# One power on GpSimd for each inverse square root, a new emission order, and other splits on GpSimd, in a fused decoder layer

## The chip, the cores and the metric

The kernel runs on one core of one Trainium2 chip. The metric is the device time of one execution in microseconds (us). The kernel before was timed in three runs: median 384.21 us, from 383.61 to 385.0.

## What is computed

One decoder layer for 256 tokens of width 1024, in fp32, cut to its steps:

```python
h = rmsnorm(x, attn_norm)                       # x: 256 x 1024
mq, mk, mv, gqkv, gz, ga, gb = split(h @ w_in)  # seven 512-wide groups, plus 8 columns
y_a = moba_attention(mq, mk, mv)                # 8 heads x 64, causal
gq, gk, gv = split(silu(causal_depthwise_conv(gqkv, conv_w)))
gq, gk = l2norm(gq) * 128**-0.5, l2norm(gk)     # l2norm: x * rsqrt(sum(x*x) + 1e-6)
o = gated_delta_rule(gq, gk, gv, log_decay, beta)   # 4 heads x 128, chunks of 64
y_b = rmsnorm(o, gdn_norm) * silu(gz)
x = x + concat(y_a, y_b) @ w_out
h = rmsnorm(x, ffn_norm)
y = hierarchical_moe(h)   # top-1 of 4 groups, top-2 of its 8 experts, gated MLP, width 256
out = rmsnorm(x + y, final_norm)
```

With 32 experts of 3 MiB the expert weights are 96 MiB; they are all read, once.

## The kernel before

**First part.** The input projection is computed with the weights cut in two fp32r halves. A weight tile of 128 x 2048 is loaded into a 1-MiB buffer; a split step S0 to S71 then takes 512 of its columns: ScalarE casts the high half (L512), and the low half is raw weight minus high half, one subtraction on VectorE or on GpSimd (L514). A string `LOW` has a letter for each split, V or G, that says which. Steps P0 to P55 are the products: each does three passes of four 128x256 matmuls (high weights by high input, high by low, low by high; L536, or L545 for one group). X.h0 to X.h7 make the two halves of the scaled input, ScalarE the high one (L432). X.d0 to X.d4 are warm-up products on zeros (L257, each lowered to two matmuls). The last sixteen splits, S56 to S71, cut the four tiles of w_out, and W0 to W7 are the output projection: 192 matmuls of 128x256 (L1209), of which each W reads its own tile half.

**Between them** stand the steps of the two mixers: the convolutions (gk, gq, gv), the norms (X.rs, K.rs, Q.rs), the inverse of the chunk matrices (I0 to I5), the recurrence (u, kv, s, p, r), its output norm and gate (ON, OG), the scores and softmax of attention (sc, sm, pt, pv). Each inverse square root of a norm is `rsqrt_steps` (L269 to L294): a bit trick and two Newton-like steps, ten or so small VectorE instructions. Users are X.rs (two chains of one column), K.rs and Q.rs (8 columns), ON0 and ON1 (`onorm`, 4 columns) and R.rs (two chains of one column). The last norm of the kernel already uses a single power instruction on GpSimd instead (L1784).

**Routing.** After the residual (X2.0 to X2.3, L1216) come the router's logits (R.lg), the ranks and one-hot choices (R.rt), the inverse root (R.rs), the dispatch matrix (M.D: `make_D` L1372, `scale_D` L1382, both 128x256 on VectorE), and the gather of the tokens for the first group (M.g, L1390). M.p is the gate product of the first group of experts (L1406).

**Experts.** Eight groups of four experts follow; for each, gate, up and down weights come in 1-MiB loads on SyncE's queue, in order, into the buffers that the first part leaves. `load_expert` issues a load where the last step that uses a buffer is emitted. One of these buffers, K1, also holds the two tiles t1x, which belong to the ring t1k of small work tiles; a step takes the ring's first free tile.

**What sets the order.** The string `ORDER` is written by hand: each word advances one step to its next yield, and so fixes the order of the instructions on every engine's own queue. Each engine runs its queue in order. Nothing reorders it afterwards.

## Time and profile before

| | us |
|---|---|
| median of 3 runs | 384.21 |
| the profiled execution | 384.3 |
| its span in the trace | 382.6 |
| TensorE (PE) busy in the span | 335.0 (88%) |
| VectorE (DVE) busy | 192.5 (50%) |
| ScalarE (ACT) busy | 105.6 (28%) |
| GpSimd (POOL) busy | 65.2 (17%) |
| moved by DMA | 123.54 MB, 322 GB/s over the span |

Shares of the whole span say little here, since the first part (up to about 170 us) and the experts have different limits; the views below go by stretch. "Idle before" in a row is the time for which the engine stood still ahead of that row's first instruction, with the instruction that ended it. Names of work tiles are those of the buffers that they share: a weight tile may be called RG, K, B, mixA or whl.

### The profile page before, as it was taken

To read this page: it belongs to the slowest core of one execution; us is meant where nothing else is said; L and a number is where in the kernel's file an instruction comes from. 1 tells how busy PE (TensorE), PEld (TensorE's weight loads), DVE (VectorE), ACT (ScalarE), POOL (GpSimd) and SP (SyncE) were. 2 spreads that over 40 slices of the span, in tenths; PEclk is the share of its full clock that TensorE was granted. 3 is DMA by queue.
4 is the path that set the end of the run, shared out by engine and by line. 5 is a ranking of instruction groups with operands and counts; after the bars stand their busy time and mean duration, and the time that the engine had idled before them with its cause. 6 is when DMAs were issued, how large, how long until landed. Compare 5 with 4: busy or idle time off the path is not lost.

```text
span 382.6 us, 8189 instructions
## 1 busy us (share of the span) xinstructions
PE 335.0 (88%) x3410; PEld 257.8 (67%) x3410; DVE 192.5 (50%) x494; ACT 105.6 (28%) x260; POOL 65.2 (17%) x106
## 2 busy tenths in 40 slices
PE   3999999999999989899969899898987697578980
PEld 2999998987878879799755656465553254254550
DVE  2798889989687876436331313223230121051543
ACT  4664555626632452304001010101010001001032
POOL 5416040630572033400000000000000000000033
PEclk9999999999999999998999999999999699899997
DMA  6979454494303856969999999999999999999952
GB/s 215 423 289 368 173 218 182 164 370 169 111 0 118 325 191 256 409 270 408 386 408 424 421 420 416 420 421 423 419 421 420 421 423 420 421 416 421 421 207 110
DMA packets 18326, 123.54 MB, mean 323 GB/s; under 512 B 2288, under 2 KB 2544, under 8 KB 3824
## 3 DMA queue, kind: packets, MB, share of 16 engines
q1 hardware_dynamic: 18288, 123.01, 79.6%
q8 instruction: 27, 0.44, 0.5%
q14 instruction: 11, 0.09, 0.1%
HBM read 121.95 MB, written 1.05 MB: 322 GB/s over the span
## 4 chain that ended last, share of the span: by engine, by line
PE 45%; DMA 42%; DVE 6%; ACT 2%; issue 1%; POOL 1%; POOLq 0%; SPq 0%; DVEq 0%; ACTq 0%
PE bank L536 18%; DMA EX<-in_w_up_dram 10%; PE bank L1209 6%; DMA hL<-in_w_gate_dram 5%; DMA whl<-in_w_down_dram 5%; DMA mixB<-in_w_down_dram 5%; DMA EX<-in_w_gate_dram 5%; DMA B<-in_w_dl_dram 5%; DMA B<-in_w_gate_dram 5%; PE bank L545 3%; PE bank L1406 3%; PE bank L1390 2%; PE bank L886 1%; PE bank L906 1%; PE bank L1700 1%
## 5 line engine op out<-in xcount | busy, mean ns | idle before, releaser
L1406 PE MATMUL bank<-EX,B2a 128*32 128x256 f32 x416 | 42.8, 396 | 5.0 <-DMA EX<-in_w_up_dram 3.6
L1406 PE MATMUL bank<-B,B2a 128*32 128x256 f32 x240 | 42.2, 395 | 3.3 <-DMA B<-in_w_gate_dram 3.3
L1705 ACT CAST B2b<-bank 128x256 fp32r<-128x256 f32 (+1 forms) x33 | 12.1, 366 | 118.8 <-PE bank L1700 104.4
L1745 POOL TENSOR_TENSOR K<-K,whl 128x256 f32<-128x256 f32 (+1 forms) x10 | 5.9, 624 | 208.4 <-DMA mixB<-in_w_dl_dram 207.4
L536 PE MATMUL bank<-hH,whl 128*128 128x256 f32 x192 | 32.5, 294 | 4.7 <-ACT whl L512 4.7
L1706 DVE TENSOR_TENSOR B2b<-bank,B2b 128x256 fp32r<-128x256 f32 (+1 forms) x33 | 13.8, 417 | 36.2 <-ACT B2b L1705 29.4
L536 PE MATMUL bank<-hL,whl 128*128 128x256 f32 x192 | 31.9, 290 | 0.0
L536 PEld LDWEIGHTS bank<-hH,whl 128*128 128x128 f32 x192 | 27.3, 197 | 6.2 <-ACT whl L512 5.6
L1406 PEld LDWEIGHTS bank<-EX,B2a 128*32 128x32 f32 x416 | 20.6, 114 | 15.2 <-DMA EX<-in_w_up_dram 4.5
L1700 PE MATMUL bank<-B,t1k 128*32 128x512 f32 (+1 forms) x104 | 26.6, 564 | 2.5 <-DVE t1k L1688 1.8
L1390 PE MATMUL bank<-t1k,B 128*128 128x128 f32 x224 | 26.9, 278 | 1.4 <-DVE t1k L1382 1.4
L1390 PEld LDWEIGHTS bank<-t1k,B 128*128 128x128 f32 x224 | 25.5, 192 | 3.8 <-issue 2.1
L536 PEld LDWEIGHTS bank<-hL,whl 128*128 128x128 f32 x192 | 26.9, 196 | 0.9 <-issue 0.8
L1406 PE MATMUL bank<-K,B2a 128*32 128x256 f32 x144 | 25.9, 404 | 1.7 <-DMA K<-in_w_up_dram 1.7
L1712 PEld LDWEIGHTS bank<-B2b,t1k 128*128 128x128 f32 x132 | 18.2, 188 | 12.3 <-ACT B2b L1705 5.9
L1712 PE MATMUL bank<-B2b,t1k 128*128 128x256 f32 (+1 forms) x132 | 24.5, 311 | 1.1
L1612 DVE TENSOR_TENSOR t1k<-t1k,late 128x256 f32<-128x256 f32 x8 | 3.4, 426 | 43.2 <-PE bank L1610 43.2
L1406 PEld LDWEIGHTS bank<-B,B2a 128*32 128x32 f32 x240 | 18.7, 113 | 8.8 <-DMA B<-in_w_gate_dram 4.3
L1393 DVE TENSOR_TENSOR B2a<-bank,late 128x512 f32<-128x512 f32 x16 | 11.1, 692 | 19.8 <-PE bank L1390 19.8
L512 ACT CAST whl<-RG 128x512 fp32r<-128x512 f32 x30 | 17.7, 614 | 9.2 <-DMA RG<-in_w_in_dram 3.7
L1659 DVE SCALAR_TENSOR_TENSOR t1k<-t1k,late,bank 128x256 f32<-128x256 f32 x8 | 3.8, 480 | 29.5 <-PE bank L1406 29.5
L514 DVE TENSOR_TENSOR mixA<-RG,whl 128x512 fp32r<-128x512 f32 x22 | 16.4, 763 | 2.8 <-ACT whl L512 2.8
(391 smaller groups left out, 767.5 us busy)
## 6 DMA issues: line engine op xcount, KB each, us to landing
EX<-in_w_up_dram SPq DMA_DIRECT2D x16, 1024.0 KB, 18.8
B<-in_w_gate_dram SPq DMA_DIRECT2D x11, 1024.0 KB, 19.3
B<-in_w_down_dram SPq DMA_DIRECT2D x11, 1024.0 KB, 19.8
EX<-in_w_gate_dram SPq DMA_DIRECT2D x10, 1024.0 KB, 10.6
EX<-in_w_down_dram SPq DMA_DIRECT2D x6, 1024.0 KB, 19.9
B<-in_w_in_dram SPq DMA_DIRECT2D x5, 1024.0 KB, 5.0
RG<-in_w_in_dram SPq DMA_DIRECT2D x5, 1024.0 KB, 4.8
K<-in_w_gate_dram SPq DMA_DIRECT2D x5, 1024.0 KB, 19.9
```

The costliest lines, as they stand in the source:

```text
L512: S.copy(out=hv, in_=src)
L514: (G if LOW[i] == "G" else V).tensor_tensor(out=lv, in0=src, in1=hv.bitcast(FP32), op=ALU.subtract)
L536: PE.matmul(o_, lhsT=a_[:, c4, j * P:(j + 1) * P], rhs=b_[:, c, :], start=(c == 0 and j % 2 == 0 and n == 0), stop=(c == KC - 1 and j % 2 ...
L545: PE.matmul(ps[tt], lhsT=a_[:, c, tt * P:(tt + 1) * P], rhs=b_[:, c4, :], start=(c == 0 and n == 0), stop=(c == KC - 1 and n == 2))
L1209: PE.matmul(o_, lhsT=a_[:, c, :], rhs=b_, start=(i == 0 and c % 2 == 0 and n == 0), stop=(i == 7 and c % 2 == 1 and n == 2), skip_group_ch ...
L1390: PE.matmul(ps[:, c4 * P:(c4 + 1) * P], lhsT=x2[tt][:, q * 4 + c4, :], rhs=Dsv[:, tt], start=(tt == 0), stop=(tt == 1))
L1393: V.tensor_tensor(out=xeT[:, q * 4:q * 4 + 4, :], in0=ps.rearrange("p (c s) -> p c s", c=4), in1=ffnT[:, q * 4:q * 4 + 4].unsqueeze(2).bro ...
L1406: PE.matmul(ps[r, 0:FF], lhsT=xeT[:, c, r], rhs=w[c // 2][0][:, c % 2, q, :] if mixed else w[q][0][:, c, :], start=(c == 0), stop=(c == KC ...
L1700: PE.matmul(ps[r, 0:w], lhsT=hv[:, ft, r], rhs=rhs, start=(ft == 0), stop=(ft == 1), tile_position=(0, q * 32))
L1705: S.copy(out=hi, in_=ps)
L1706: V.tensor_tensor(out=lo, in0=ps, in1=hi.bitcast(FP32), op=ALU.subtract)
L1712: PE.matmul(ps[tt][:, 0:w], lhsT=DwT[:, tt * P:(tt + 1) * P], rhs=ye[k], start=(first and k == 0), stop=(grp >= NG - 2 and k == 1), skip_g ...
```

## The change

1. `rsqrt_steps` and its interleaver are gone. `inv_root(dst, v, n)` takes their place: one power with exponent -0.5 on GpSimd, of 128 x n values. X.rs and R.rs do both columns in one instruction (n = 2), K.rs and Q.rs have n = 8, ON0 and ON1 n = 4 each. Of VectorE's queue 477 rows become 412 (some rows stand for two or more instructions).
2. `ORDER` is another string: other places for nearly all steps ahead of the experts. The five warm-ups X.d all stand ahead of the first product; E0 to E5, which load expert weights into spare buffers, come at other places, E1 among them.
3. `LOW` has 23 letters G in the place of 14.
4. Routing takes its small tiles with `take(True)`, which skips the two tiles t1x in K1.

```diff
-LOW = "VVVVVVVVVVVVVVVVVVVVVVVVVVVVGVVVVVVVVVGGVGVGGGVVVVVVVGGGVVVVVGVVVGGGVVVV"
+LOW = "VVVVVVVVVVVVVVVVVVGVVVVVVVVVVVVGVGGVVVVGVGGGGVGGGVVGVGGVGVVVGVGGVGGVVVGG"
...
-        def take(self):
+        def take(self, own=False):
             assert self.q, "no free buffer"
-            return self.q.popleft()
+            i = 0
+            while own and any(self.q[i] is b for b in t1x):
+                i += 1
+            t = self.q[i]
+            del self.q[i]
+            return t
...
-    def rsqrt_steps(dst, v, n, sml=None):
...
+    def inv_root(dst, v, n):
+
+        G.tensor_tensor(out=dst, in0=v, in1=mhalf.broadcast_to([P, n]), op=ALU.pow)
...
-        yield from inter(*[rsqrt_steps(rstd[:, tt:tt + 1], ssq[:, 3 + tt:4 + tt], 1) for tt in range(2)])
+        inv_root(rstd, ssq[:, 3:5], 2)
...
-        yield from inter(rsqrt_steps(rk, ssk, 8))
+        inv_root(rk, ssk, 8)
...
-        yield from inter(rsqrt_steps(rq, ssn, 8))
+        inv_root(rq, ssn, 8)
...
-            yield from inter(rsqrt_steps(ro, mo, 4))
+            inv_root(ro, mo, 4)
...
-        for tt in range(2):
-            V.tensor_scalar(out=ss2[:, 2 * tt:2 * tt + 1], in0=ss2[:, 2 * tt:2 * tt + 1], scalar1=1e-6, scalar2=None, op0=ALU.add)
-            yield
-        yield from inter(*[rsqrt_steps(rs2[:, tt:tt + 1], ss2[:, 2 * tt:2 * tt + 1], 1, LATE) for tt in range(2)])
+        ms2 = ss2.rearrange("p (t q) -> p t q", q=2)[:, :, 0]
+        V.tensor_scalar(out=ms2, in0=ms2, scalar1=1e-6, scalar2=None, op0=ALU.add)
+        yield
+        inv_root(rs2, ms2, 2)
```

(`take(True)` stands in R.k, `rank`, R.rt, `make_D` and `scale_D`.)

Line numbers of the changed kernel are lower by some 29 past `inv_root`. On TensorE's queue the start of the kernel before is this (L257 is the warm-up, one row for two matmuls; L536 a product of P0):

```order
L257 MATMUL bank_67<-EX_95 128x256
L257 MATMUL bank_68<-EX_95 128x256
L257 MATMUL bank_69<-EX_95 128x256
L536 MATMUL bank_70<-hH,whl_100 128x256 x2
L536 MATMUL bank_71<-hH,whl_100 128x256 x2
L536 MATMUL bank_70<-hL,whl_100 128x256 x2
```

and of the changed kernel (L261 the warm-up, L507 the product):

```order
L261 MATMUL bank_67<-EX_95 128x256
L261 MATMUL bank_68<-EX_95 128x256
L261 MATMUL bank_69<-EX_95 128x256
L261 MATMUL bank_70<-EX_95 128x256
L261 MATMUL bank_71<-EX_95 128x256
L507 MATMUL bank_72<-hH,whl_100 128x256 x2
L507 MATMUL bank_73<-hH,whl_100 128x256 x2
```

Two warm-ups moved up from later places between products, so that five stand in front.

On GpSimd's queue around the output projection, the kernel before has the last output norm work (L1144), the low half of a mixer output (L1093), the router's scaled weights (L1272) and four splits of w_out (L514):

```order
L1144 TENSOR_TENSOR K_58<-K_58,K_60 128x512 x2
L1093 TENSOR_TENSOR mixA<-B2b,mixA 128x4x128 x2
L1272 TENSOR_TENSOR B_82<-K_60,late 128x288
L514 TENSOR_TENSOR whl_101<-K_59,whl_101 128x512
L514 TENSOR_TENSOR whl_100<-RG_89,whl_100 128x512
L514 TENSOR_TENSOR whl_101<-RG_89,whl_101 128x512 x2
```

and the changed kernel, with L271 the power, L485 the split, L1064 the mixer output, L1243 the router's weights and L1256, L1258 routing constants:

```order
L271 TENSOR_TENSOR K_60<-K_60,late 128x4 x2
L1115 TENSOR_TENSOR K_58<-K_58,K_60 128x512
L485 TENSOR_TENSOR B_1578<-RG_89,B_1578 128x512
L1064 TENSOR_TENSOR mixA<-B2b,mixA 128x4x128 x2
L1243 TENSOR_TENSOR B_82<-K_60,late 128x288
L485 TENSOR_TENSOR whl_101<-K_59,whl_101 128x512
L485 TENSOR_TENSOR B_1660<-K_59,B_1660 128x512 x2
L1256 MEMSET t1k_77 128x64
L485 TENSOR_TENSOR whl_101<-RG_89,whl_101 128x512
L485 TENSOR_TENSOR whl_100<-RG_89,whl_100 128x512
L1258 AFFINE_SELECT t1k_77<-t1k_77 128x64
L485 TENSOR_TENSOR whl_100<-K_59,whl_100 128x512 x2
```

Behind the mixer's output, four splits became seven, and one stands ahead of it.

On SyncE's queue, the loads of the second group's experts begin in the kernel before with

```order
L473 DMA B_80<-in_w_down_dram 128x2048 [waits DMAHW2_49,DVE_49]
L473 DMA K_60<-in_w_down_dram 128x2048 [waits DMAHW3_49]
L470 DMA K_58<-in_w_gate_dram 128x2048 [waits DMAHW4_49,DVE_49,PE_49]
L470 DMA B_79<-in_w_gate_dram 128x2048 [waits DMAHW5_49,PE_49]
```

and in the changed one with

```order
L444 DMA B_80<-in_w_down_dram 128x2048 [waits DMAHW2_49,DVE_49]
L444 DMA K_60<-in_w_down_dram 128x2048 [waits DMAHW3_49]
L441 DMA K_58<-in_w_gate_dram 128x2048 [waits DMAHW4_49]
L441 DMA B_79<-in_w_gate_dram 128x2048 [waits DMAHW5_49,PE_49]
```

The load into K1 (K_58) lost its waits for VectorE and TensorE; the load behind it kept its wait.

## Rows read from the trace of the kernel before

**Rows 1.** By stretch: busy PE, PEld, DVE, ACT, POOL (instructions), PE clock, DMA share, GB/s.

```profile
9.00:53.00 44.00, 44.00 (x358) 43.13 (x359) 35.86 (x94) 23.95 (x51) 13.23 (x35) 1.00 0.76 300
...
61.00:112.00 51.00, 50.97 (x630) 44.50 (x629) 44.13 (x107) 25.28 (x62) 21.01 (x20) 1.00 0.48 186
...
204.00:369.00 165.00, 139.37 (x1512) 84.09 (x1514) 43.49 (x95) 14.91 (x42) 0.16 (x1) 0.97 1.01 417
```

**Rows 2.** Timeline of TensorE, start: start, duration, line, operation, idle before.

```profile
8.92 1.22 PE L536 MATMUL bank<-hH,whl 128*128 128x256 f32 x4 [4.73 <-ACT whl L512]
...
13.57 0.64 PE L536 MATMUL bank<-hH,whl 128*128 128x256 f32 x4
...
23.35 0.60 PE L257 MATMUL bank<-EX 128*128 128x256 f32 x2
23.60 0.82 PE L536 MATMUL bank<-hH,whl 128*128 128x256 f32 x4
```

**Rows 3.** Timeline of ScalarE, just ahead of the first product.

```profile
6.66 1.70 ACT L432 ACTIVATE hH<-B,K 128x256 fp32r<-128x256 f32 x4
```

**Rows 4.** Timeline of TensorE, two waits between the projections and the mixers.

```profile
60.31 0.74 PE L536 MATMUL bank<-hH,mixA 128*128 128x256 f32 x4 [0.68 <-DVE mixA L514]
...
142.21 0.76 PE L1179 MATMUL bank<-B 128*64 128x256 f32 x3 [1.12 <-DVE B L1164]
```

**Rows 5.** Timeline of TensorE, the output projection, with the instruction behind it.

```profile
143.99 1.21 PE L1209 MATMUL bank<-mixA,B 128*128 128x256 f32 x6
...
147.55 3.40 PE L1209 MATMUL bank<-mixA,whl 128*128 128x256 f32 x27
150.79 1.30 PE L1209 MATMUL bank<-mixA,B 128*128 128x256 f32 x9
...
159.76 0.86 PE L1209 MATMUL bank<-mixB,whl 128*128 128x256 f32 x5 [0.97 <-POOL whl L514]
...
162.01 1.94 PE L1209 MATMUL bank<-mixB,whl 128*128 128x256 f32 x14 [0.55 <-DVE whl L514]
...
169.91 1.31 PE L1238 MATMUL bank<-B,B2a 128*128 128x36 f32 x11
```

**Rows 6.** Timeline of GpSimd in the output projection.

```profile
158.43 2.98 POOL L514 TENSOR_TENSOR whl<-RG,whl 128x512 fp32r<-128x512 f32 x2 [3.34 <-ACT whl L512]
```

**Rows 7.** The split's line by engine: count, shortest/median/longest ns, first to last start.

```profile
L514 DVE TENSOR_TENSOR mixA<-RG,whl x22: 642/686/1534, 8.9 to 114.7; 128x512 fp32r<-128x512 f32 x22
...
L514 POOL TENSOR_TENSOR mixB<-B,whl x5: 1272/1295/1555, 52.5 to 97.3; 128x512 fp32r<-128x512 f32 x5
```

**Rows 8.** Timelines of VectorE and of GpSimd, a split beside a GpSimd operation.

```profile
56.30 1.81 DVE L514 TENSOR_TENSOR mixB<-B,whl 128x512 fp32r<-128x512 f32 x1
...
56.28 1.28 POOL L757 TENSOR_TENSOR B<-K,K 128x512 f32<-128x512 f32 x1
```

**Rows 9.** Timeline of VectorE, first and last of one Newton chain's ten instructions.

```profile
125.08 0.17 DVE L282 TENSOR_SCALAR K<-K 128x4 int32<-128x4 int32 x1
...
126.50 0.17 DVE L293 SCALAR_TENSOR_TENSOR K<-K 128x4 f32<-128x4 f32 x1
```

**Rows 10.** GpSimd: the last norm's power (timeline), and a multiplication (groups by line).

```profile
375.80 0.72 POOL L1784 TENSOR_TENSOR late<-late 128x2 f32<-128x2 f32 x1
...
L823 POOL TENSOR_TENSOR K<-K 128x8 f32<-128x8 f32 x1 | 0.2, 203 | 11.3 <-DVE K L821 11.3
```

**Rows 11.** Timeline of VectorE, routing: the scaled dispatch matrix.

```profile
180.07 0.43 DVE L1382 TENSOR_TENSOR K<-t1k,late 128x256 f32<-128x256 f32 x1
```

**Rows 12.** SyncE's queue, timeline: issues of expert loads.

```profile
164.69 0.33 SPq L470 DMA_DIRECT2D K<-in_w_up_dram  x1
...
184.48 0.33 SPq L470 DMA_DIRECT2D K<-in_w_gate_dram  x1
188.05 0.33 SPq L470 DMA_DIRECT2D B<-in_w_gate_dram  x1
```

**Rows 13.** DMA in one 3-us stretch: length, granted TensorE clock, DMA share, GB/s.

```profile
189.00:192.00 3.00, 1.00 0.97 317
```

More of the change, by code (lines that the diff above doesn't have):

```diff
@@ L73 @@
[L73 to L76 removed]
+C.b*4 X.d1 C.d C.b*2 X.d0 C.b X.h1 C.b X.h0 X.h1 X.h3 X.d3 X.d2 X.h0 C.b*3 X.d4 S0 P0*2 S1 X.h3 S2 S0 P0 C.a S1 X.h2*2 C.b*2 X.h4*2 X.h5*2 S3 P1*3 P2
@@ L77 @@
+R.s11 R.rs R.rt sm4 G.cum R.c00 R.rt R.rs R.d*3 R.c01 R.c10 R.rs R.c11 R.rt M.D*2 M.g0*3 M.w*2 M.g1*3 M.p*4 M.w*9 sm1 K.A sm5 R.d*2 M.w*9
 """
-LOW = "VVVVVVVVVVVVVVVVVVVVVVVVVVVVGVVVVVVVVVGGVGVGGGVVVVVVVGGGVVVVVGVVVGGGVVVV"
+LOW = "VVVVVVVVVVVVVVVVVVGVVVVVVVVVVVVGVGGVVVVGVGGGGVGGGVVGVGGVGVVVGVGGVGGVVVGG"
 @with_exitstack
@@ L263, in hybrid_layer_kernel @@
     G.memset(bones[64:128, 64:128], 1.0)
-    def rsqrt_steps(dst, v, n, sml=None):
-        sml = sml or K3
-        vh, va, tq, ya = (sml(n) for _ in range(4))
-        yi = sml(n, dt=I32)
-        a = 0.375 ** 0.5
-        def times(y, w):
-            if n == 1:
-                V.scalar_tensor_tensor(out=tq, in0=y, scalar=w, in1=y, op0=ALU.mult, op1=ALU.mult)
-            else:
-                V.tensor_tensor(out=tq, in0=y, in1=y, op=ALU.mult)
-                yield
-                V.tensor_tensor(out=tq, in0=tq, in1=w, op=ALU.mult)
-            yield
-        V.tensor_scalar(out=yi, in0=v.bitcast(I32), scalar1=-0.5, scalar2=float(0x5F3759DF - 2 ** 31), op0=ALU.mult, op1=ALU.add)
-        V.tensor_scalar(out=va, in0=v, scalar1=a, scalar2=None, op0=ALU.mult)
-        V.tensor_scalar(out=vh, in0=v, scalar1=0.5, scalar2=None, op0=ALU.mult)
-        yield
-        y = yi.bitcast(FP32)
-        yield from times(y, va)
-        V.scalar_tensor_tensor(out=tq, in0=tq, scalar=-1.25 / a, in1=tq, op0=ALU.add, op1=ALU.mult)
-        yield
-        V.scalar_tensor_tensor(out=ya, in0=tq, scalar=1.875, in1=y, op0=ALU.add, op1=ALU.mult)
-        yield
-        yield from times(ya, vh)
-        V.scalar_tensor_tensor(out=dst, in0=tq, scalar=-1.5, in1=ya, op0=ALU.add, op1=ALU.mult)
-        yield
-    def inter(*chains):
-        chains = list(chains)
-        while chains:
-            chains = [ch for ch in chains if next(ch, 0) is None]
-            if chains:
-                yield
+    def inv_root(dst, v, n):
+        G.tensor_tensor(out=dst, in0=v, in1=mhalf.broadcast_to([P, n]), op=ALU.pow)
     def run(*chains):
-        for _ in inter(*chains):
-            pass
+        for chain in chains:
+            for _ in chain:
+                pass
     tri = K2(P)
@@ L1275, in _ @@
     def _():
-        rt["k"] = k = t1k.take()
+        rt["k"] = k = t1k.take(True)
         triS = k[:, 0:P]
@@ L1295, in rank @@
     def rank(rk_, val, n):
-        tg = t1k.take()
+        tg = t1k.take(True)
         gt, df = (view(tg, o_, 2, n, n) for o_ in (0, 128))
@@ L1312, in _ @@
     def _():
-        b = rt["b"] = t1k.take()
+        b = rt["b"] = t1k.take(True)
         at = [0]
@@ L1368, in make_D @@
     def make_D(grp, src):
-        Dg = t1k.take()
+        Dg = t1k.take(True)
         es = slice(grp * EG, grp * EG + EG)
@@ L1378, in scale_D @@
     def scale_D(grp):
-        Ds = t1k.take()
+        Ds = t1k.take(True)
         Dsv, Dv = (view(t, 0, 2, EG * CAP) for t in (Ds, Dgs[grp][0]))
@@ L1783, in hybrid_layer_kernel @@
         V.scalar_tensor_tensor(out=ms[:, tt:tt + 1], in0=ss3[:, tt, NL - 1:NL], scalar=1.0 / D, in1=ms[:, tt:tt + 1], op0=ALU.mult, op1=ALU.add)
-    G.tensor_tensor(out=rs3, in0=ms, in1=mhalf.broadcast_to([P, 2]), op=ALU.pow)
+    inv_root(rs3, ms, 2)
     S.activation(out=xf[:, 1, 0:CUT], in_=xf[:, 1, 0:CUT], func=AF.Copy, scale=rs3[:, 1:2])
```

45 lines of the change are left out of this document (20 added, 25 removed).

## The prediction

> **What bounds the kernel now.** I read the busy time by stretch first [rows 1]. Between 9 and 53 us TensorE is busy 44.00 of 44 us, between 61 and 112 us 50.97 of 51: the first part is bound by TensorE, and time can be won only from the few places where it stands still, runs slowly, or does work that need not be there. From 204 to 369 us it is the other way round: the DMA share is 1.01 at 417 GB/s, so the experts' weights are the limit, and the end comes when the last byte has landed. The two are tied by the loads' issue times [rows 12]: eight expert loads, of which the first is issued at 164.69, are let go one after the other by the last products of the output projection, the load into K1 follows at 184.48, and the one behind it at 188.05 when a gate product has read its buffer. So whatever makes the first part and routing shorter moves these issues, and with them the end, by the same amount. Whatever lies after 190 us can win nothing.
>
> Then I looked in TensorE's timeline for what it loses. At the start [rows 2] the 24 products between 8.92 and 13.57 take 4.65 us, 0.19 each, though 0.12 is what one takes later (27 products from 147.55 to 150.79, 3.24 us [rows 5]); 24 at 0.12 would be 2.88, so 1.77 us are lost there, right behind 4.73 us without work. The granted clock reads full speed in this stretch, so the row shows the slowness and not its reason. In the middle there are two waits worth naming, 0.68 and 1.12 us [rows 4]. The output projection runs from 143.99 to 169.91 [rows 5], 25.92 us for 192 products of which each takes 0.12: 23.04, so 2.88 lost; the two named waits in it, 0.97 for GpSimd and 0.55 for VectorE, and the restarts behind them, lie where two splits on GpSimd, begun at 158.43 on a late cast, take 2.98 us [rows 6].
>
> **The change, part by part, against the profiled execution of 384.3 us** (its span is 382.6, and 1.7 lie around it; it stands 0.1 above the median, so the sum can be read against either).
>
> *Start.* The order puts three scaled-input steps ahead of the first split where there were four; four of ScalarE's take 1.70 us [rows 3], so one fewer is 0.43 us: the first product comes about 0.4 earlier. And all five warm-ups, ten matmuls where there were six, now stand in the gap ahead of it. If what TensorE did before sets the speed of the first products, some of the 1.77 us comes back; I take half, 0.8, since a part of the gap remains. Sum −1.2, from 0 (neither) to −2.2 (all).
>
> *Two warm-ups* leave the packed queue. One costs 0.25 us there (23.35 to 23.60 [rows 2]), and no wait stands beside it: −0.5. This has one answer.
>
> *Waits in the middle.* The new order can remove 0 to 1.80 us [rows 4]; I take half, −0.9. These waits stand in front of a split's low half and of a copy, both on VectorE, which loses 72 instructions of its queue.
>
> *Output projection.* Of 2.88 us lost I expect 2.0 back. In the new order TensorE does all of W4 ahead of W5, and the low halves for the last landed tile are shared out over more time. What is late next: three splits on GpSimd behind the last landing, where two took 2.98 us. Bounds 0 and −2.88.
>
> *Inverse roots.* A Newton chain on 8 or 4 columns takes from 125.08 to 126.67, 1.59 us [rows 9]. The power has one row: 0.72 us for two columns; a multiplication of 8 columns takes 0.20 [rows 10], so a column of power costs an estimated 0.26 ((0.72 − 0.20) / 2), four cost 1.24 and eight 2.28. The bounds are 0.72 (no cost by column) and 4 × 0.72 = 2.88. So 8 columns come 0.7 us later (from −0.9 to +1.3), 4 columns 0.35 us earlier. TensorE has products of the projections to do meanwhile, since the first part is packed [rows 1]: I take 0 for all five ahead of the output projection. If that cover is gone, K.rs and Q.rs cost 0.7 each and at worst 2.6 together.
>
> *R.rs.* Here nothing covers it, but it isn't the only thing that `scale_D` (180.07 [rows 11]) waits for: the ranks and `make_D` are ready only some 0.3 us earlier. The power, issued some 0.15 us after the sums with 0.72 for itself, is ready before `make_D` ends. −0.3, from 0 to −0.4.
>
> *K1's load* loses its wait for VectorE and TensorE. It was issued at 184.48, but eight loads issued since 164.69 are 8 MiB, 20 us of transfer at 417 GB/s, so the queues had work up to about 184.7, and the load behind it still waits for the gate product at 188.05 [rows 12]. The shortfall that shows in DMA is 317 against 417 GB/s for 3 us, 0.72 us [rows 13], and it comes after that later load. I take 0, bounds 0 and −0.7.
>
> *Nine more splits on GpSimd.* This is the price. A split takes 0.69 us on VectorE and 1.29 on GpSimd [rows 7], so a low half that TensorE needs next comes 0.6 us later. And while GpSimd runs an operation on two inputs, VectorE's split beside it takes 1.81 us and not 0.69 [rows 8]: 1.12 more. A split that is wanted at once thus costs 1.72 us; one with time to spare costs nothing, and relieves VectorE of 0.69. Nine in all would be 15.5 us, none would be 0. VectorE has 6.9 us to spare between 61 and 112 us [rows 1], and most of these splits stand there or in the output projection, well ahead of their products; I take one as late: +1.7.
>
> Here a rule speaks against the change. The Trainium skill, "GPSIMD Engine Reference", section 4.1, Engine selection, gives elementwise work on a tile to VectorE and calls GpSimd about two times slower on two inputs; its section 8, Key points, adds that the two share their ways into SBUF, with contention where a VectorE instruction has two inputs there. The trace agrees with both: 1.29 against 0.69, and 1.81 beside an operation on GpSimd. By the rule as it stands none of the nine should have moved. It leaves out what a packed VectorE queue costs its neighbours, and so what it would give here is the fourth case below.
>
> The sum without the last term is −1.2 − 0.5 − 0.9 − 2.0 − 0.3 = −4.9, which gives 379.4; each late split adds 1.72: one 381.1, two 382.8, three 384.6, four 386.3.
>
> **The cases.** *Forecast: one or two late splits, or none,* 379.4 to 382.8, with 381.1 in the middle. For it: VectorE is 81% busy from 9 to 53 and 87% from 61 to 112 us [rows 1], so it has room for a neighbour's contention, and GpSimd is at 30 to 41% there. *All waits go and the start is full speed:* 384.3 − 2.2 − 0.5 − 1.8 − 2.9 − 0.3 = 376.6. For it speaks that each loss has a named cause of its own in the queues; against it, that a tile of w_out still lands when it lands. *The gain is eaten by new waits:* three late splits, 384.6, or the same from fewer and from the two powers of 8 columns (381.1 + 2.6 = 383.7). *GpSimd becomes the bound in the output projection, and the kernel is slower:* there GpSimd has seven splits behind the mixer's output where it had four; at 1.49 each (half of 2.98 [rows 6]) that is 10.4 us against 6.0, and the last three follow the last landing. Nothing stands on TensorE's queue behind W7 that could fill a wait, and routing and every load hang on it. From four splits that are late (4 × 1.72 = 6.9, more than the 4.9 won) the kernel is slower; with four it is 386.3. *The change doesn't do what it says:* GpSimd's power could be slow on a strided or 8-column operand, or the buffers that loads wait for could be freed no earlier because another step now uses them last; then the −2.5 of projection, routing and a part of the waits is missing and 383 to 384.5 is left. That is in the third case.
>
> **How the numbers follow.** Chances: forecast 0.55; all waits gone 0.12; eaten 0.15; slower 0.18. Predicted is the forecast's middle, 381.1. The range of 8 in 10 goes from 377.2, which leaves out about half of the case of 376.6, to 386.0, which leaves out somewhat more than half of the slower case. The bound within which this kernel can't be told from no change is about 0.3%, 1.15 us either way (383.1 to 385.4 on the median). The forecast and the full gain lie below it, the eaten case inside or just at its edge, the fourth above: faster 0.68, same 0.14, slower 0.18; the 0.02 moved from the forecast are for two late splits with nothing else won.
>
> **What would show each step.** Start: the first product earlier than 8.92, and 0.12 per product from fewer than 24 products on; if the slow stretch is as long as before, the half is wrong. Warm-ups: no L261 row after the first product. Output projection: from its first product to the router's first in 23.5 to 24.5 us; a wait for GpSimd over 2 us there is the fourth case. Powers: five rows on GpSimd, two of 8 columns near 2.3 us, two of 4 near 1.2; waits of TensorE right behind a power mean that the cover was not there. Routing: `scale_D` some 0.3 us sooner after the last sum of squares. Split contention: VectorE's splits of 1.7 us and more, counted against the few in the trace of before; if TensorE's waits named "split" add up to over 5 us in the stretch up to 140 us, the last term is wrong. The end: the expert loads as full as before, 417 GB/s, and the last landing earlier by the same as the end of the output projection; if it isn't, the tie between the two parts is wrong.

## The result, and the profile after

The changed kernel takes 380.7 us in the median of 14 runs, the kernel before 383.62 in as many on the same chip: a ratio of 0.9918, with a 95% interval from 0.9900 to 0.9937. One execution of 539.83 us at a mean granted clock of 0.55 is left out of the ratio, as are one execution of e6 and two of e8 below, each over 1.5% above its kernel's fastest; the others here lie between 377.91 and 382.95. Against the profiled execution of before, 384.3 us, the ratio gives 381.1, the predicted time; the range held it. The profiled execution of the changed kernel is 381.01 us, its span 379.3, so 3.3 us less than before. Where these 3.3 us come from is not where the prediction's sum had them.

By stretch, as in [rows 1] (start and end, length, busy time of TensorE, its weight loads, VectorE, ScalarE and GpSimd, granted clock, DMA share, GB/s):

```profile
9.00:53.00 44.00, 41.72 (x345) 40.70 (x344) 32.15 (x68) 23.41 (x50) 16.31 (x37) 0.97 0.86 339
...
61.00:112.00 51.00, 49.52 (x646) 43.10 (x640) 45.05 (x92) 24.47 (x60) 27.50 (x23) 1.00 0.42 159
...
157.00:162.00 5.00, 5.00 (x44) 5.00 (x43) 3.00 (x3) 2.43 (x5) 3.68 (x5) 1.00 1.02 433
162.00:170.00 8.00, 8.00 (x71) 8.00 (x69) 2.58 (x4) 0.00 (x0) 0.36 (x3) 1.00 0.99 387
```

TensorE, which had no idle time from 9 to 53 us, now loses 2.28 us there, and 1.48 us between 61 and 112; from 157 to 170 it has no gap. Its timeline names the places, and answers to [rows 2], [rows 4] and [rows 5]:

```profile
1.25 4.08 PE L261 MATMUL bank<-EX 128*128 128x256 f32 x10 [1.25 <-DVE EX L250]
8.12 1.22 PE L507 MATMUL bank<-hH,whl 128*128 128x256 f32 x4 [2.79 <-ACT whl L483]
...
29.58 0.74 PE L507 MATMUL bank<-hH,mixA 128*128 128x256 f32 x4 [2.29 <-DVE mixA L485]
...
73.01 1.15 PE L857 MATMUL bank<-B,B 64*64 64x64 f32 x32 [0.97 <-DVE B L847]
...
141.51 0.65 PE L1150 MATMUL bank<-B 128*64 128x256 f32 x2 [0.61 <-DVE B L1135]
142.50 0.43 PE L1150 MATMUL bank<-B 128*64 128x256 f32 x1 [0.34 <-DVE B L1135]
...
143.94 0.50 PE L1180 MATMUL bank<-mixA,B 128*128 128x256 f32 x2
145.02 0.74 PE L1180 MATMUL bank<-mixA,B 128*128 128x256 f32 x4 [0.57 <-POOL mixA L1064]
...
167.91 1.87 PE L1209 MATMUL bank<-B,B2a 128*128 128x36 f32 x16
...
178.80 3.81 PE L1361 MATMUL bank<-t1k,B 128*128 128x128 f32 x32 [1.13 <-DVE t1k L1353]
```

The first product comes 0.80 us earlier, yet the output projection starts at 143.94 where it started at 143.99: all that was won ahead of it is lost again ahead of it. It then lasts 23.97 us and not 25.92. From its end to the gather it is 10.89 us where it was 10.73. So the gather starts 1.84 us earlier, and the rest of the 3.3 must lie behind it. Two views show it. SyncE's queue, one load of the kernel before (the other is the first of [rows 12]), then the changed kernel:

```profile
165.53 0.33 SPq L470 DMA_DIRECT2D RG<-in_w_up_dram  x1
```

```profile
159.25 0.33 SPq L441 DMA_DIRECT2D RG<-in_w_up_dram  x1
162.03 0.33 SPq L441 DMA_DIRECT2D K<-in_w_up_dram  x1
...
170.49 0.44 SPq L441 DMA_DIRECT2D K<-in_w_gate_dram  x1
186.21 0.33 SPq L441 DMA_DIRECT2D B<-in_w_gate_dram  x1
```

The load into RG, issued at 165.53, now goes out at 159.25, and the load into K, issued at 164.69, at 162.03. And DMA by stretch (granted clock, share, GB/s), first of the kernel before, then of the changed one:

```profile
156.00:162.00 6.00, 1.00 1.01 425
162.00:168.00 6.00, 1.00 0.50 195
168.00:198.00 30.00, 0.94 0.99 397
```

```profile
156.00:162.00 6.00, 1.00 1.01 426
162.00:168.00 6.00, 1.00 1.01 419
168.00:198.00 30.00, 0.94 0.96 388
```

Between 162 and 168 us the kernel before moved 195 GB/s, the changed one 419: 1.34 MB more, 3.2 us of transfer at 420 GB/s. From 168 to 198 it moves 0.27 MB less (0.6 us). From 204 to 360 us both move 420 GB/s, so a lead in bytes is kept. Counted by bytes, the two traces are level at 38 MB (162.2 and 162.3 us); at 39 MB the changed kernel is 3.2 us ahead, by 50 MB it has given 0.7 to 0.8 of that back, and from there to 121 MB it stays some 2.5 us ahead. So 2.5 of the 3.3 us are what is left of the hole. The other 0.8 come at the very end, with the last loads; why isn't shown.

The fourteen traces of this study fit that: the bytes moved by 204 us go from 50.96 MB (e7, a span of 388.0 us) to 55.81 (e11, 376.6), and a straight line through all fourteen, 2.2 us per MB, misses no span by more than 1.3 us. The hole alone does not decide. e8 has none (414 GB/s from 162 to 168), but it is 1.0 MB behind the kernel before at 162 us and moves 382 GB/s from 168 to 198 where that one moves 397; by 204 us both have moved nearly the same (53.35 and 53.54 MB), and their spans are 383.2 and 382.6. No run moves the two loads alone, so that the closed hole makes the gain is read from traces and not shown by an experiment. Bytes moved by a given time tell more here than any engine's busy share.

### The profile page after: what moved, and what is told of

The parts are those of the page before. It is cut to its first block, busy times and chain, and to the rows that moved or that the text cites. A ratio compares the mean times of both kernels' runs of the same rounds, so it can differ in the third digit from the quotient of the medians.

```text
span 379.3 us, 8138 instructions
## 1 busy us (share of the span) xinstructions
PE 335.2 (88%) x3410; PEld 258.1 (68%) x3410; DVE 181.4 (48%) x412; ACT 105.5 (28%) x260; POOL 85.2 (22%) x121
## 4 chain that ended last, share of the span: by engine, by line
DMA 50%; PE 32%; DVE 9%; POOL 3%; issue 2%; ACT 2%; SPq 1%; POOLq 0%; DVEq 0%; ACTq 0%
DMA EX<-in_w_up_dram 10%; DMA RG<-in_w_in_dram 7%; PE bank L1180 6%; DMA mixB<-in_w_down_dram 5%; DMA hH<-in_w_gate_dram 5%; DMA whl<-in_w_down_dram 5%; DMA B<-in_w_dl_dram 5%; DMA hL<-in_w_gate_dram 5%; PE bank L507 4%; DMA B<-in_w_gate_dram 4%; PE bank L516 3%; PE bank L1377 3%; PE bank L1361 2%; DMA B<-in_xt_dram 2%; DVE mixA L485 2%
## 5 line engine op out<-in xcount | busy, mean ns | idle before, releaser
L1377 PE MATMUL bank<-B,B2a 128*32 128x256 f32 x272 | 43.5, 403 | 2.2 <-DMA B<-in_w_gate_dram 2.2
L1676 ACT CAST B2b<-bank 128x256 fp32r<-128x256 f32 (+1 forms) x33 | 12.1, 366 | 117.0 <-PE bank L1671 102.5
L507 PE MATMUL bank<-hH,whl 128*128 128x256 f32 x192 | 31.8, 291 | 2.8 <-ACT whl L483 2.8
L1361 PE MATMUL bank<-t1k,B 128*128 128x128 f32 x256 | 30.7, 278 | 2.6 <-DVE t1k L1353 2.6
L1361 PEld LDWEIGHTS bank<-t1k,B 128*128 128x128 f32 x256 | 29.2, 192 | 5.1 <-issue 2.1
L507 PE MATMUL bank<-hL,whl 128*128 128x256 f32 x192 | 31.4, 287 | 0.0
L1377 PE MATMUL bank<-EX,B2a 128*32 128x256 f32 x352 | 28.5, 404 | 1.9 <-DMA EX<-in_w_up_dram 1.9
L507 PEld LDWEIGHTS bank<-hH,whl 128*128 128x128 f32 x192 | 27.0, 197 | 4.0 <-ACT whl L483 3.2
L507 PEld LDWEIGHTS bank<-hL,whl 128*128 128x128 f32 x192 | 26.7, 194 | 0.3 <-issue 0.2
L1683 PE MATMUL bank<-B2b,t1k 128*128 128x256 f32 (+1 forms) x132 | 24.5, 312 | 1.1
L1671 PE MATMUL bank<-B,t1k 128*32 128x512 f32 (+1 forms) x88 | 23.0, 558 | 1.6 <-DVE t1k L1659 0.9
L1377 PEld LDWEIGHTS bank<-EX,B2a 128*32 128x32 f32 x352 | 14.3, 116 | 8.6 <-DMA EX<-in_w_up_dram 2.8
L507 PE MATMUL bank<-hH,mixA 128*128 128x256 f32 x96 | 16.1, 291 | 2.3 <-DVE mixA L485 2.3
L1671 PE MATMUL bank<-EX,t1k 128*32 128x512 f32 x80 | 14.6, 596 | 3.6 <-DVE t1k L1659 3.6
```

The source lines that it names most:

```text
L507: PE.matmul(o_, lhsT=a_[:, c4, j * P:(j + 1) * P], rhs=b_[:, c, :], start=(c == 0 and j % 2 == 0 and n == 0), stop=(c == KC - 1 and j % 2 ...
L1361: PE.matmul(ps[:, c4 * P:(c4 + 1) * P], lhsT=x2[tt][:, q * 4 + c4, :], rhs=Dsv[:, tt], start=(tt == 0), stop=(tt == 1))
L1377: PE.matmul(ps[r, 0:FF], lhsT=xeT[:, c, r], rhs=w[c // 2][0][:, c % 2, q, :] if mixed else w[q][0][:, c, :], start=(c == 0), stop=(c == KC ...
L1671: PE.matmul(ps[r, 0:w], lhsT=hv[:, ft, r], rhs=rhs, start=(ft == 0), stop=(ft == 1), tile_position=(0, q * 32))
L1676: S.copy(out=hi, in_=ps)
L1683: PE.matmul(ps[tt][:, 0:w], lhsT=DwT[:, tt * P:(tt + 1) * P], rhs=ye[k], start=(first and k == 0), stop=(grp >= NG - 2 and k == 1), skip_g ...
```

## The experiments

All ratios are against the kernel before, run beside them (its median there was 383.36 to 383.96). Two readings of every trace serve for all: the output projection's first product and its length, and the gather's start. A trace is of one execution, which can lie well off its median (e1's took 385.14 us, e6's 385.43).

| run | median us | ratio, 95% interval | projection starts, lasts | gather |
|---|---|---|---|---|
| before | 383.62 | 1 | 143.99, 25.92 | 180.64 |
| changed | 380.7 | 0.9918 (0.9900 to 0.9937) | 143.94, 23.97 | 178.80 |
| e1_t1x_in_scale | 381.15 | 0.9930 (0.9904 to 0.9956) | 145.10, 23.98 | 179.97 |
| e2_before_own | 383.92 | 0.9995 (0.9970 to 1.0020) | 143.93, 25.91 | 180.51 |
| e3_s16_later | 380.3 | 0.9912 (0.9880 to 0.9944) | 142.52, 23.97 | 176.24 |
| e4_gap_filled | 382.06 | 0.9943 (0.9922 to 0.9964) | 144.86, 23.97 | 178.56 |
| e5_before_pow | 383.44 | 1.0005 (0.9981 to 1.0029) | 143.56, 25.91 | 180.07 |
| e6_after_newton | 381.9 | 0.9955 (0.9927 to 0.9982) | 146.15, 23.96 | 180.40 |
| e7_after_old_low | 388.63 | 1.0136 (1.0103 to 1.0170) | 148.93, 27.54 | 187.36 |
| e8_after_old_low_wout | 384.64 | 1.0009 (0.9981 to 1.0037) | 143.38, 27.48 | 181.73 |
| e9_dummies_back | 380.39 | 0.9898 (0.9870 to 0.9926) | 143.79, 23.96 | 177.47 |
| e10_before_new_low | 386.54 | 1.0064 (1.0040 to 1.0088) | 150.41, 25.36 | 185.78 |
| e11_three_waits | 380.46 | 0.9902 (0.9879 to 0.9925) | 141.04, 23.99 | 176.27 |
| e12_three_waits_dummies | 380.28 | 0.9900 (0.9879 to 0.9921) | 142.12, 23.97 | 177.34 |

**K1's load.** Undone alone, and done alone:

```diff
 # e1_t1x_in_scale, in the changed kernel
-        Ds = t1k.take(True)
+        Ds = t1k.take()
 # e2_before_own, in the kernel before: take(own) as in the change, and take(True) at its five places
```

> The changed kernel with one call put back: scale_D takes the ring's first free tile again, which is one of the two in K1, so the load into K1 waits for VectorE and TensorE as in the kernel before. Theory A (of the 3.3 us that the trace shows, 1.4 come from this load, since from the next load's issue to the last landing it is 179.38 us where it was 180.77): K1's load is issued near 182.6, the load behind it near 186.2 as now, last landing and time 1.4 us later, about 382.1. Theory B (as the prediction had it: the load is hidden behind others, and the 1.4 come from loads of up weights issued at 159 and 162 us where it was 165): no more than 0.3 later, about 380.8.

> The kernel before with one part of the change: routing takes no tile of K1. Theory A: K1's load is issued at about 172.7 and not at 184.48, the next one at 188.05 as it was, the last landing about 1.4 us earlier, 382.2. Theory B: 383.4 to 383.8, as before.

The load went where it should: issued at 183.81 in e1, and at 172.36 in e2, where before it was 184.48:

```profile
172.36 0.67 SPq L475 DMA_DIRECT2D K<-in_w_gate_dram  x1
187.92 0.33 SPq L475 DMA_DIRECT2D B<-in_w_gate_dram  x1
```

The time of e2 did not move (0.9995), and e1 is 0.4 us above the changed kernel, well within the two intervals. Theory A falls by e2: I had read 1.4 us for this load out of one pair of traces, as the time from the next load's issue to the landing of the last expert load but two (180.7 and 179.3). Over the fourteen traces of this study that time is between 179.2 and 182.3, with no relation to K1's load: 181.67 in e2, where it goes early, 180.73 in the kernel before. One pair of profiles can't carry 1.4 us there. A few tenths for this load in the changed kernel stay open.

**The start.** In the changed kernel the cast and the low half of S16, which belong to weight tile 4 (counted from 0), stand ahead of work on tile 3 that TensorE needs sooner, and tile 4 lands only at 25.7 us: that makes about half of the wait at 29.58 (the other half is a split on GpSimd, S18, shown under the letters). e3 moves the two words (S11 and S18 shift with them); e4 fills the gap ahead of the first product with more warm-ups; e9 goes back to three.

```diff
 # e3_s16_later
-E4 S16 G.ch*8 P8 S10 P9*3 S16 S12*2 P10*2 G.ch P10 P11*2 S18 G.abT S11 P11 P7
+E4 G.ch*8 P8 S10 P9*3 S12*2 P10*2 G.ch P10 P11*2 S11 S16 G.abT P11 S16 S18 P7
 # e4_gap_filled
-        steps[f"X.d{i}"] = lambda: dummies(1)
+        steps[f"X.d{i}"] = lambda i=i: dummies(4 if i == 4 else 1)
 # e9_dummies_back
-X.h3 X.d3 X.d2 X.h0 C.b*3 X.d4 S0
+X.h3 X.d3 X.h0 C.b*3 S0
...
+X.d4 ahead of C.d S6, X.d2 ahead of P37
```

> The changed kernel with the two words S16 behind S11 in the order, so that neither ScalarE's casts of tile 3 nor VectorE's low half that P11 needs stand behind the cast of tile 4, whose load lands only at 25.8 us in the trace. Theory C (the start's gain is lost in one wait of 2.29 us at 29.58, which is this queue order): the wait is gone or under 0.7, the output projection starts 1 to 2 us earlier, the time is 378.7 to 379.7. Theory D (the weights' landings bound this stretch, so that whatever is won comes back as a wait at the next tile, or in the mixers): the output projection starts within 0.5 of 143.94, the time is 380.2 to 380.9.

> The changed kernel with eight warm-ups and not five ahead of the first product, so that TensorE is at work until about 7.8 us and not 5.3, the first product at 8.12 as now. If what TensorE did just before sets the speed of the first products, their slow stretch (16 products in 3.48 us, 1.55 lost) shrinks to under 0.5 lost. Theory D (tile 4's landing decides): the wait at 29.58 grows by as much and the time stays within 0.4 of 380.7. Theory C (the start's gain goes through to the end): 1 us earlier, 379.7.

> The changed kernel with three warm-ups ahead of the first product and two back between later products, about where the kernel before has them. The prediction's price (0.8 for the speed of the first products and 0.5 for two warm-ups in the packed queue): the output projection starts 1 us later or more, 381.7 to 382.2. Rival (the first products run at half speed for some 3.5 us with either count, and the wait for tile 4 near 29 us takes up what is lost ahead of it): the wait shrinks, one warm-up of 0.25 us is left as cost, 380.6 to 381.2.

e3: the wait at 29.58 is gone, one of 0.81 for a cast at 38.62 comes, and the output projection starts 1.42 us earlier, as theory C had it. But the median is 380.3, in the band of theory D; with six runs the interval reaches from 0.9880 to 0.9944 and can't tell a gain of one microsecond from none. e4 is plainer. TensorE's timeline there:

```profile
1.25 6.39 PE L261 MATMUL bank<-EX 128*128 128x256 f32 x16 [1.25 <-DVE EX L250]
8.05 0.74 PE L507 MATMUL bank<-hH,whl 128*128 128x256 f32 x4 [0.41 <-ACT whl L483]
...
29.38 0.74 PE L507 MATMUL bank<-hH,mixA 128*128 128x256 f32 x4 [3.25 <-DVE mixA L485]
...
31.98 1.05 PE L507 MATMUL bank<-hH,whl 128*128 128x256 f32 x4
```

The first products do run faster when TensorE was at work until just before: the first 24 take 3.15 us here (8.05 to 11.20), 0.13 each, and 4.43 in the changed kernel. And all of it is lost again, since the wait at 29.38 grows from 2.29 to 3.25, ending at nearly the same time. Tile 4 lands at 25.47 us here and at 25.67 in the changed kernel, and in both ScalarE, which has stood idle for 4.6 us or more, then makes tile 4's cast ahead of those that are needed sooner. Beyond that e4 has a stretch at half clock (products of 0.21 near 32 us). Its median is 1.4 us above the changed kernel's, outside the bands of both theories, with intervals that overlap. e9, with three warm-ups, is no slower than the changed kernel with five (0.9898; the median of 380.39 lies below the rival's band, and far from the prediction's price): the wait behind it is 1.28 and not 2.29. The start's gain of about a microsecond, and the half microsecond for the two warm-ups, do not show at the end.

**The powers.** Done alone in the kernel before (the power where the chain began, its other yields kept empty), and undone alone in the changed one:

```diff
 # e5_before_pow, five places like this one
-        yield from inter(rsqrt_steps(rk, ssk, 8))
+        yield from inv_root(rk, ssk, 8, 8)   # one G.tensor_tensor(op=pow), then 8 yields
 # e6_after_newton: inv_root issues the whole Newton chain on VectorE, the last norm's power kept
```

> The kernel before with one part of the change: each inverse root of the first part is one power on GpSimd, put where the Newton chain began, the order of all else and the split letters as before. The prediction's price (nothing ahead of the output projection, 0.3 us won in routing): output projection starts within 0.3 of 143.99, scale_D 0.3 earlier after the last sum of squares, 383.3 to 383.6. Rival (powers of 8 columns are late, 0.7 us each on the path): output projection starts up to 1.4 later, 384.3 to 385.

> The changed kernel with its new order and letters, but each inverse root a Newton chain on VectorE again, all its instructions at the place of the power. If the powers are worth nothing by themselves ahead of the output projection: it starts within 0.3 of 143.94 and only routing is longer, by 0.3 to 0.7, since the 16 small instructions now stand ahead of make_D: 381.0 to 381.4. Rival (taking 72 instructions from VectorE's packed queue is what makes the new order possible): the output projection starts 1 us later or more, 382 or more.

By themselves the powers are worth nothing that can be measured (1.0005). In e5's trace the output projection starts 0.43 us earlier, of an execution whose first product also came 0.76 earlier. In the new order going back to Newton costs 1.2 us in the median (0.9955 against 0.9918, intervals that overlap, so the size is not shown). The trace of e6, of the slowest of its twelve executions, shows two places: a wait of 1.54 us behind the chain of Q.rs, and the 16 small instructions ahead of `make_D`. VectorE there (the chain's first and slowest steps, and its last):

```profile
113.72 0.17 DVE L283 TENSOR_SCALAR K<-K 128x8 int32<-128x8 int32 x1
...
114.96 1.29 DVE L280 TENSOR_TENSOR K<-K 128x8 f32<-128x8 f32 x1
116.28 0.17 DVE L294 SCALAR_TENSOR_TENSOR K<-K 128x8 f32<-128x8 f32 x1
```

From the rank's products to the gather it is 2.54 us (177.86 to 180.40), where e9 has 1.98 (175.49 to 177.47): 0.56 for routing. So neither expectation holds in full: routing as in the first; ahead of the output projection, which starts 2.2 us later in this trace, as in the rival, whose 382 or more the median just misses.

**The letters.** All old letters in the new order, the old ones for w_out alone, and all new letters in the old order:

```diff
 # e7_after_old_low, changed kernel
-LOW = "VVVVVVVVVVVVVVVVVVGVVVVVVVVVVVVGVGGVVVVGVGGGGVGGGVVGVGGVGVVVGVGGVGGVVVGG"
+LOW = "VVVVVVVVVVVVVVVVVVVVVVVVVVVVGVVVVVVVVVGGVGVGGGVVVVVVVGGGVVVVVGVVVGGGVVVV"
 # e8_after_old_low_wout: the same for the last sixteen letters; e10_before_new_low: the reverse of e7, in the kernel before
```

> The changed kernel with the split letters of the kernel before, 14 on GpSimd and not 23. If the nine more splits on GpSimd cost one late split of 1.7 us (the prediction's last term) and nothing else: output projection starts 1 to 2 us earlier. If the letters belong to the new order and take load off VectorE where it binds: VectorE's waits ahead of 143 us grow by 1 us or more, or the output projection takes 1 us longer than 23.97, 381.5 or more. If they matter to neither: 380.4 to 381.0.

> The changed kernel with the old letters only for the sixteen splits of w_out, so that S56, S60, S62, S63, S70, S71 are on VectorE and S61, S67 on GpSimd. If the order (all of W4 ahead of W5) is what shortened the output projection from 25.92 to 23.97 us: it stays within 0.4 of 23.97, 380.5 to 381.1. If the letters did it, with VectorE free for the last tile: it takes 25 us or more, and the time is 381.5 to 382.7.

> The kernel before with the new split letters, 23 on GpSimd and not 14, in its old order. Theory E (letters and order belong together; the nine more splits hurt where the order doesn't fit them, as the old letters hurt the new order): VectorE's and GpSimd's waits grow, output projection 25.9 us or longer, 384.5 to 389. Rival F (the letters of w_out alone shorten the output projection): it takes 24 to 24.5 us and the time is 381.5 to 382.5.

This is where the change lives. Nine more on GpSimd is the net count: fifteen letters went from V to G and six from G to V. With the old letters the new order is 8 us slower than with its own, 1.4% slower than the kernel before; with the old letters for w_out alone nearly 4 us, and the whole gain is gone; that is slower than either expectation of e8 had. In the old order the new letters cost 2.6 us (386.54 against 383.96 beside it), as theory E had it. e7's trace has its loss in two places: between 61 and 112 us TensorE stands idle for 4.16 us and not 1.48, mostly in waits for VectorE, and the output projection, which starts 4.99 us later, lasts 3.57 longer. e8 shows the second place alone. GpSimd's queue, then TensorE's:

```profile
141.81 1.28 POOL L485 TENSOR_TENSOR whl<-K,whl 128x512 fp32r<-128x512 f32 x1 [6.35 <-ACT whl L483]
143.05 3.38 POOL L1064 TENSOR_TENSOR mixA<-B2b,mixA 128x512 fp32r<-128x512 f32 x2
```

```profile
143.38 0.50 PE L1180 MATMUL bank<-mixA,B 128*128 128x256 f32 x2
146.48 0.74 PE L1180 MATMUL bank<-mixA,B 128*128 128x256 f32 x4 [2.60 <-POOL mixA L1064]
...
147.41 3.82 PE L1180 MATMUL bank<-mixA,B 128*128 128x256 f32 x18
151.07 2.68 PE L1180 MATMUL bank<-mixA,whl 128*128 128x256 f32 x21
```

One split too many stands on GpSimd ahead of the mixer's output, for which TensorE's queue waits at its third product: 2.60 us of wait where the changed kernel has 0.57. That split is S61, one of the six that the new string gives back to VectorE (there it runs at 143.15, 0.69 us). So at this place the new letters win by a split taken off GpSimd and not by one put there. And behind that wait the granted clock falls to half, 1.2 GHz (0.50 from 147.6 to 150.9 us), so that 18 products take 3.66 us and not 2.16. Wait and clock are 2.0 and 1.5 us, which is the whole of 27.48 against 23.97. That S61 alone would do it was not run. From 151 on e8's projection has no gap either: the stalls that the kernel before had behind its last tile [rows 5] are taken out by the order, and the letters keep the start of the projection free. e10 shows the price in the old order, on VectorE and TensorE:

```profile
57.49 1.79 DVE L514 TENSOR_TENSOR mixB<-B,whl 128x512 fp32r<-128x512 f32 x1
...
60.65 1.77 DVE L514 TENSOR_TENSOR mixB<-B,whl 128x512 fp32r<-128x512 f32 x1
62.34 1.75 DVE L514 TENSOR_TENSOR mixA<-RG,whl 128x512 fp32r<-128x512 f32 x1
```

```profile
64.14 1.22 PE L536 MATMUL bank<-hH,mixA 128*128 128x256 f32 x4 [3.74 <-DVE mixA L514]
```

Three of VectorE's splits lie beside GpSimd's and take 1.75 to 1.79, and TensorE waits 3.74 us for the last. That is the prediction's slower case, in the order to which the letters do not belong. (This trace is of the slowest of its eight runs, so its later times are not those of the median.) The changed kernel pays that price once too, at the start: VectorE's split that ends the wait at 29.58 lies beside S18, which the new string gives to GpSimd.

```profile
27.71 1.26 POOL L485 TENSOR_TENSOR mixA<-RG,whl 128x512 fp32r<-128x512 f32 x1 [0.53 <-ACT whl L483]
...
27.75 1.77 DVE L485 TENSOR_TENSOR mixA<-EX,whl 128x512 fp32r<-128x512 f32 x1
```

With S18 on VectorE, in e7, that split takes 0.68 us from 27.69, and the wait is 1.12 us and not 2.29:

```profile
28.43 0.74 PE L507 MATMUL bank<-hH,mixA 128*128 128x256 f32 x4 [1.12 <-DVE mixA L485]
```

**A faster version.** Three of TensorE's waits in the changed kernel have a short way out: S16 later, as in e3, and two subtractions on VectorE where it stood waiting for GpSimd.

```diff
 # e11_three_waits, on top of e3; e12_three_waits_dummies: with e9's warm-ups too
-        G.tensor_tensor(out=TU[:, 0], in0=idb, in1=a0, op=ALU.subtract)
+        V.tensor_tensor(out=TU[:, 0], in0=idb, in1=a0, op=ALU.subtract)
-            G.tensor_tensor(out=mixA[:, 1, :, ts], in0=ov,
+            (V if tt == 0 else G).tensor_tensor(out=mixA[:, 1, :, ts], in0=ov,
```

> The changed kernel with S16 later, as in the run of that name, and two subtractions moved from GpSimd to VectorE where VectorE stands idle for them: that of I0.a (1.40 us on GpSimd, 1.18 of it VectorE's idle time, ahead of a wait of TensorE of 1.24) and the second low half of the mixer's output (1.82 us beside a split, ahead of a wait of 0.58 in the output projection's start). If a wait removed is time won, since nothing else is late there: the first wait shrinks to 0.5 or less, the second to under 0.2, output projection starts 0.7 us earlier than with S16 alone and is 0.5 shorter, the time is 378.7 to 379.4. Rival (the loads' landings take up what is won): 380 to 380.6.

> As the run with the three waits removed, and with three warm-ups ahead of the first product as in the run with the warm-ups put back. If five warm-ups let the granted clock fall to half a second time near 30 us in some executions (as in two traces), and three do not: spread narrower, median 0 to 0.5 lower. If not: 0 to 0.5 higher, by the two warm-ups in the queue.

In e11's trace the wait ahead of I0.a's products (0.97 us in the changed kernel's trace, 1.24 in e3's) is gone and the output projection starts at 141.04, 2.90 us before the changed kernel's and 1.48 before e3's. The second did not go as expected: the wait for the mixer's low half is still 0.61, now for VectorE. e12's runs spread as much (379.4 to 381.49) as e11's (378.57 to 380.68), so its warm-ups decide nothing either. The medians are 380.46 and 380.28, the ratios 0.9902 and 0.9900, 0.2 of a per cent better than the changed kernel's, with intervals that overlap it. Both versions beat the kernel before; that they beat the changed one isn't shown, and most of the 2.9 us that e11 wins ahead of the output projection in its trace (an execution of 378.57 us, the fastest of its six) does not arrive in the median, which lies in the rival's band. A part of it goes in routing: from the projection's end to the gather it is 11.24 us in e11, with a stretch at half clock from 168.5 to 171.8, and 9.75 in e3, with none, so that e11's gather (176.27) is no earlier than e3's (176.24). Where the rest goes isn't settled.

## Why the prediction was right, and where its steps were not

*The sum.* −3.2 us was forecast, −3.3 is the difference of the two profiled executions and −3.1 the ratio's. The total is right, and partly by luck. Up to the gather −3.2 was forecast and −1.84 measured; the other 1.4 to 1.5 stand in no term. The start's −1.2 did not go through, the +1.7 for more splits on GpSimd has the wrong sign for the letters as a whole, and the loads that are let go earlier were not in the sum. The chances do not add up either: the forecast and the full gain are 0.67 and the eaten case 0.15, and no 0.02 moved from the forecast makes 0.68 and 0.14 of them.

*Output projection.* −2.0 taken, −1.95 measured, 23.97 us in a forecast band of 23.5 to 24.5. Right, with the mechanism half told: the order takes the stalls out, and it needs the new letters to keep 3.5 us from coming back at the start (e8).

*Start and warm-ups.* −1.2 and −0.5 taken. The first product came 0.80 earlier. From ScalarE's first activation to it there were 2.26 us before (6.66 to 8.92) and 2.02 after (6.10 to 8.12), so 0.24 and not 0.43 is the one activation fewer; the other 0.56 is when the first loads landed, which differs by as much between executions (the first product is at 8.16 to 8.92 in four traces of the old order). Of the slow products 0.22 came back and not 0.8: the 25th product is at 12.55 and not 13.57. The prediction read a full clock there. That reading was empty: the trace of before holds no clock record ahead of 12.77 us, and the views count time without a record as full. The products speed up at that point, from 0.21 us each (11.64 to 12.50) to 0.12 (13.10 to 13.57), as they do in the changed kernel, where the granted clock is 0.50 from 8.1 to 11.4 us and 1.00 behind that. None of the start's gain went through: the step that failed is that time won at the start is won at the end. Behind it stands a tile that lands at 25.5 (e4) or 25.8 us (e9), in a stretch in which DMA was at 415 GB/s, with a cast that the new order puts ahead of others and a split slowed by GpSimd's S18; I had put none of them into the sum at this place. With that cast later (e3), 1.42 us do reach the output projection.

*Waits in the middle.* −0.9 taken, and +1.7 for one late split. The wait of 0.68 at 60.31 is gone, that of 1.12 at 142.21 is 0.95 in two pieces, and 2.29, 0.97, 0.51 and 0.36 are new (two of them in the rows above). All that stands ahead of the output projection was forecast at −0.9 and measured −0.05.

*Nine more splits on GpSimd.* For the letters as a whole the sign is wrong. The term's arithmetic is sound: e10 shows it at work, 1.75 to 1.79 us for a split beside GpSimd, and so does S18 in the changed kernel, with 1.2 us of wait where 1.7 were taken. But the sum lets each late split add 1.72 and counts no win, though the text names the 0.69 by which a split relieves VectorE; it took the old order's queue for the new one's, and the net of nine for the change. In the new order the letters as a whole, fifteen to GpSimd and six back, win 8 us (e7). The rule weighed in the prediction (the Trainium skill, "GPSIMD Engine Reference", section 4.1, Engine selection, and section 8, Key points, on the shared ways into SBUF) shows its two sides here: e10 agrees with it, and so do S18 and S61 in the new order; e7's longer waits for VectorE between 61 and 112 us speak against it. In these runs what a split costs on either engine depended on the queue that it stood in. The two times of a lone split, 0.69 and 1.29 [rows 7], are again in the trace after:

```profile
L485 DVE TENSOR_TENSOR mixA<-RG,whl x16: 677/686/693, 8.4 to 118.7; 128x512 fp32r<-128x512 f32 x16
...
L485 POOL TENSOR_TENSOR mixA<-RG,whl x8: 1263/1287/1532, 27.7 to 114.6; 128x512 fp32r<-128x512 f32 x8
```

*Inverse roots.* 0 taken ahead of the output projection; e5 agrees; e6's trace, of its slowest execution, points to some worth there in the new order, and its size is not shown. The power's own cost, estimated at 1.24 and 2.28 us for 4 and 8 columns, is 1.01 and 1.65 to 1.78 in the changed kernel (8 columns took 2.17 and 2.65 in e5):

```profile
66.24 1.78 POOL L271 TENSOR_TENSOR K<-K,late 128x8 f32<-128x8 f32 x1 [1.91 <-DVE K L762]
...
107.78 1.65 POOL L271 TENSOR_TENSOR K<-K,late 128x8 f32<-128x8 f32 x1
...
130.40 1.01 POOL L271 TENSOR_TENSOR K<-K,late 128x4 f32<-128x4 f32 x1 [3.50 <-DVE K L1035]
```

*R.rs.* −0.3 taken, and right at its own place: from the last sum of squares on VectorE to `scale_D` it was 2.31 us (177.76 to 180.07 [rows 11]) and is 2.03.

```profile
177.76 0.21 DVE L1355 TENSOR_SCALAR late<-late 128x1 f32<-128x1 f32 x1 [0.30 <-ACT B L1253]
```

```profile
176.20 0.21 DVE L1326 TENSOR_SCALAR late<-late 128x1 f32<-128x1 f32 x1 [1.15 <-ACT B L1224]
...
178.23 0.42 DVE L1353 TENSOR_TENSOR t1k<-t1k,late 128x256 f32<-128x256 f32 x1
```

The whole of routing, from the projection's end to the gather, is +0.16 in the pair. Both executions had a stretch at half clock near 173 us, and in the changed kernel's VectorE then waits 1.15 us for the last square and not 0.30. In traces without that stretch the old routing takes 10.01 us (e10) and the new one 9.72 to 9.75 (e3, e4, e9): the −0.3 again. The power alone saves 0.13 in the old order (10.60 in e5 against 10.73).

*K1's load.* 0 taken, with the reason that the load behind it waits anyway; e2 bears it out.

*What was missing.* The prediction said that eight loads are let go by the last products of the output projection. For the first two that was wrong: they wait for the last splits of two tiles of w_out. The last split of the tile in K ended at 164.66 in the kernel before, the load into K following at 164.69 and that into RG behind it; in the changed kernel it ends at 162.00, the load at 162.03, and the tile in RG was done at 159.15:

```profile
163.97 0.69 DVE L514 TENSOR_TENSOR whl<-K,whl 128x512 fp32r<-128x512 f32 x1 [2.02 <-ACT whl L512]
```

```profile
158.89 3.11 POOL L485 TENSOR_TENSOR whl<-K,whl 128x512 fp32r<-128x512 f32 x2 [1.32 <-ACT whl L483]
```

The cast ahead of it had to wait for TensorE until 163.32 before and until 159.54 after, so TensorE's products free a buffer for it earlier. The two loads go out 3 and 6 us ahead of the old issue. That fills the hole from 162 to 168, 3.2 us of transfer of which 2.5 are left at the end, out of 1.95 us of TensorE's time. It is the term that replaced the start's.

## What to carry to other kernels

When the end is set by a saturated transfer, ask of a reordering which buffer it frees earlier and count the bytes moved by a fixed time, late enough that all kernels run at the same rate from there on. Time won on the busiest engine is worth nothing while a later step, such as a cast that stands in its queue ahead of a load's landing, takes it up again. The price of an operation on another engine holds only for the queue in which it was measured, and a net count of moved operations hides those that were moved back; test an assignment and an order crosswise (new with old, old with new) before calling either good or bad. Where executions of one kernel scatter by 1%, one pair of traces proves only what is fixed by the program's order, such as the length of a stage without transfers, and that only at the same clock.
